# Casts of operands moved behind copies out of PSUM, and one set of block sums moved by one output block

## The chip, the cores and the metric

The kernel runs on one core of one Trainium2 chip. The metric is the device time of one execution in microseconds, as a median of several runs. One execution is also taken with the hardware profiler, and its trace gives the views that are quoted here.

## The reference, cut to what matters

Two layers over a stream `x` of 1024 tokens by 1024 channels. In layer 0 the output of two mixer branches goes through an output projection, is scaled by a gate and added to `x`. Layer 1 is the pooling mixer; in it stands most of what the change touches:

```python
def odd_mixer(h, p, on_grid):
    z = h @ p["w_in"]
    u, g = jnp.split(z, [W_POOL], axis=-1)          # 2048 columns each
    d = multiscale_pool(u ...)                      # windows of 2, 4, 8, 16 along a row of 64
    y = jnp.einsum("bngi,gij->bngj", d, p["w_grp"]) * p["scale"]
    return (y * jax.nn.silu(g)) @ p["w_out"]        # 2048 -> 1024

x = x + gate[:, None] * out_x                       # per layer
return rmsnorm(x, final_g)
```

All is float32, to float32 accuracy.

## The kernel before

**Layout.** Channels lie on the 128 partitions and tokens on the free axis, so a tile of 128 channels is 128x1024, in two halves of 512 (`HALF`). 1024 channels are 8 tiles (`KT`), the 2048 of the pooling mixer 16 (`NK`).

**Three products for one.** A float32 operand is cut into a high part, which is a cast to the fast format `fp32r` on ScalarE, and a low part, which is the operand less the high part, on VectorE (`split`, L101 to L103). `prod` (L985) multiplies high by high, high by low and low by high: 4 k-tiles by 3, 12 matmuls of 128x512 for a product.

**Seven products for eight.** From the output projection of layer 0 on, a pair of output column tiles is one block, made by `quad` (L1000). It treats weights and operand as 2x2 matrices of blocks and makes seven products (a Strassen-Winograd scheme). The operand's seven sums are called `BOPS = ("b11", "t1", "t2", "b21", "t3", "b22", "t4")`. `quad` issues the products in the order b11, t1, t2, b21, t3, b22, t4 into three PSUM banks `a`, `c` and `b` (in the trace `qa_`, `qc_`, `qb_` with the block's name). After the first, ScalarE copies `a` into `b` (L1005), because the products of t2, t3 and t4 are added on top of it. Wherever a part of the block is complete, `put(i, h, x, part)` takes it out of PSUM. For the second row of the block (`i == 1`) `put(1, 1, ...)` has to copy `b` out on ScalarE (L1483 in the gate blocks, `copied`, L1538, in the output blocks) before the product of t4 may go on adding to `b`. `keep_part` (L1031) copies first halves of sums into SBUF (L1033).

**The stages that matter here, in the order of the trace.** `woa` is the half of layer 0's output projection that goes over branch A: 4 blocks from about 686 us on, with operands `ya`. Then, for each pair of the 16 column tiles of the pooling mixer, a value block `v` and a gate block `g` (until about 1125 us). Then the output projection of the mixer in two parts of 1024 rows: blocks `wo0_0`, `wo0_2`, `wo0_4`, `wo0_6` with the operands of part 0 (`yops[0]`), and `wo1_0` and on with those of part 1.

**Operands of the mixer's output.** `y`, the mixer's values times the gate, comes out one pair of column tiles at a time. `y_keep` (L1405) stores the pair's blocks b11, b21 and b22 to memory; `y_sums` (L1410) makes t1 to t4 with four VectorE instructions (`block_sums`, L912 to L916) and stores them; `y_operand` (L1415) loads an operand again and splits it. `y_sums` of a pair runs one pair later; that of the last pair (14 and 15) runs inside a `put` of `wo0_0`.

**What sets the order.** A planner orders the instructions of each engine by a simulated time line and by priorities: an instruction's number in the program, less `EVAC = 1000` inside `tc.high_priority`. So what stands in a `put` is moved ahead of nearly all else when its inputs are there. `tc.issue_after(x)` puts the instructions that are written inside it behind `x` in the order of `x`'s engine. Each engine then works through its list in order. So does SP, which issues nearly all transfers: one that waits for a free tile holds up those behind it.

**Tiles that are shared.** Tiles come from pools with a fixed number of slots. The `d` pool has 16 tiles of 128x1024 and holds, around the first output blocks, the operands b11, b21 and t4 of part 0 (four tiles each), the last two column tiles y14 and y15, and weights. The `v` pool has two tiles of 128x512: the residuals of the output blocks' second row (`xp`, loaded at L1549) and the third sum of `y_sums` (`yt3`) take turns in it. A pair of raw weight tiles (`wr`) is loaded at L955 and freed when its splits are done. The ring gives block `wo0_2` the tiles wh, wl, d, d, wh, wl, d for its seven weight sums.

Of the kernel before, what the change touches and what calls it, by code (L numbers as in the profile page):

```python
# [55 lines left out]
def body(ctx, tc, xT, ctxT, cc, ccol, modT, modW, win, gw, wout, wu, grp, wg, wo1, small, edge, ident, outT):  # L56
    nc = tc.nc
# [849 lines left out]
    def split_op(ops, name, i, src):  # L907
        hi, lo = ops[name]
        return split(src, hi[i], lo[i], nc.vector)
# [87 lines left out]

    def quad(w, name, ops, put, ahead=None):  # L1000
        p1, p2, p3, p4, p5, p6, p7 = w
        a, c, b = psum(f"qa_{name}"), psum(f"qc_{name}"), psum(f"qb_{name}")
        prod(a, p1, ops["b11"], True, False)
        with tc.high_priority(offset=EVAC):
            evac = nc.scalar.copy(b, a)  # L1005
        prod(c, p5, ops["t1"], True, False)
        with tc.high_priority(offset=EVAC):
            put(1, 1, c, 0)
        prod(b, p6, ops["t2"], False, False)
        with tc.high_priority(offset=EVAC):  # L1010
            put(0, 1, b, 0)
        prod(a, p2, ops["b21"], False, True)
        with tc.high_priority(offset=EVAC):
            put(0, 0, a, None)
        w = None
        if ahead is not None:
            with tc.issue_after(evac.ins):
                w = ahead()
        prod(b, p7, ops["t3"], False, False)
        with tc.high_priority(offset=EVAC):  # L1020
            put(1, 1, b, 1)
        prod(c, p3, ops["b22"], False, True)
        with tc.high_priority(offset=EVAC):
            put(0, 1, c, 1)
        prod(b, p4, ops["t4"], False, True)
        with tc.high_priority(offset=EVAC):
            put(1, 0, b, None)
        return w


    def keep_part(parts, name, i, x):  # L1031
        parts[i] = ttile(f"s{i}_{name}")
        nc.scalar.copy(parts[i], x)  # L1033

    def wr_tile(name):
        return wpool.tile([P, D], F32, tag="wr", name=name)
# [214 lines left out]
    w0 = w0()  # L1251
    for name in BOPS[4:]:
        operand(ya, name, dtile, "ya")
        for i in range(KH):
            split_op(ya, name, i, kept[name][i])

    x1 = [None] * KT
    nacc = [atile("n1acc0"), atile("n1acc1")]
# [9 lines left out]
    def woa(m, w, ahead):  # L1268
        for q in range(2):
            x1[m + q] = xtile(f"x1_{m + q}")  # L1270

        def put(i, h, x, part):
            v, dr = x1[m + i][:, HALF[h]], x1_part[m + i][:, HALF[h]]
            if part != 1:
                nc.sync.dma_start(v, dr)
            nc.vector.scalar_tensor_tensor(out=v, in0=x, scalar=m0[:, 0, 2 * KT + m + i : 2 * KT + m + i + 1],
                                           in1=v, op0=mult, op1=add)
            if part != 0:
                nc.sync.dma_start(dr, v)
                square_acc(nacc[h][:, :H], v, (m, i) == (0, h), f"n1q{m}_{i}_{h}")  # L1280
        return quad(w, f"woa{m}", ya, put, ahead)

    idD = cH[:, :P]
    nc.sync.dma_start(idD, ident)
# [127 lines left out]
        for name in ("t1", "t2", "t3", "t4"):  # L1412
            y_store(m, name, t[name])

    def y_operand(ops, part, name, raw_tile, alloc):  # L1415
        hi, lo = [], []
        for q in range(2):
            if raw_tile is not None:
# [4 lines left out]
            if raw_tile is None:  # L1423
                r = lo[q].bitcast(F32)
                nc.sync.dma_start(r, y_raw[part][name][:, q * S : (q + 1) * S])
            split(r, hi[q], lo[q], nc.vector)
        halves = lambda ts: [t[:, h] for t in ts for h in HALF]
        ops[name] = halves(hi), halves(lo)

    yops = [{}, {}]  # L1430

    def y_operands(part, raws, names=BOPS, alloc=None):
        for name in names:
            y_operand(yops[part], part, name, next(raws),
                      alloc or (dtile if name in ("b11", "b21", "t4") else d2tile))

    def wo_ring(tags):
        def ring(name):
# [10 lines left out]
                     part == 1 and m >= KT - 4)  # L1449

    wo1_ring = wo_ring(iter(["x", "x", "x", "wh", "wl", "wh", "wl"] + ["wh", "wl", "d", "d"] * 14))
    vps, silu = [], [None]
    for m in range(0, NK, 2):
        wv = wv0 if m == 0 else v_weights(m, ring_x)
        if m == 0:
# [20 lines left out]
        def to_gate(i, h, x, part):  # L1476
# [3 lines left out]
                return  # L1480
            if part == 1:
                if i == 1:
                    nc.scalar.copy(v, x)  # L1483
                    x = v
                nc.vector.tensor_tensor(out=v, in0=x, in1=parts[i], op=add)
                x = v
# [16 lines left out]
                nc.sync.dma_start(raw, modT[1, n + q])  # L1503
                mod_tile(m1, 1, n + q, raw, (cL2,), raw)
        if m == NK - 2:
            y_operands(0, iter([dtile] + [xtile] * (4 - 1)), BOPS[:4])
        for i in range(2):
            for h in range(2):
                pool(m + i, h, vps[2 * i + h])
        w = quad(wq, f"g{m}", bx, to_gate, (lambda: wo1_weights(0, 0)) if m == NK - 2 else None)  # L1510
        if m == NK - 2:
            with tc.issue_after(silu[0].ins):
                y_operands(0, iter([xtile] * 7), BOPS[4:])
# [21 lines left out]

    def copied(name, x):
        t = ttile(f"b_{name}")
        nc.scalar.copy(t, x)  # L1538
        return t

    for m in range(0, KT, 2):
        parts = {}

        def put(i, h, x, part):
# [11 lines left out]
                x = s  # L1556
            gated(m + i, t, x)
            nc.sync.dma_start(x1_part[m + i][:, HALF[h]], t)
            if (m, i, h) == (0, 0, 1):
                y_sums(NK - 2)  # L1560
        def nxt():
            if m < KT - 2:
                with tc.issue_after(stored[0].ins):
                    return wo1_weights(0, m + 2)
            w = wo1_weights(1, 0)
            y_operands(1, iter([xtile]), BOPS[3:4])
            return w

        if m == KT - 2:
            with tc.issue_after(loaded[0].ins):  # L1570
                y_operands(1, iter([xtile] * 2), BOPS[1:3])
        w = quad(w, f"wo0_{m}", yops[0], put, nxt)
        if m == 2:
            with tc.issue_after(loaded[0].ins):
                y_operands(1, iter([xtile]), BOPS[:1], lambda name, dt: xtile(name, dt))
    def x2_load(m):
        with tc.issue_after(loaded[0].ins):
# [299 lines left out]
```

## Time and profile before

| | |
|---|---|
| median of 3 runs | 1294.53 us (1294.15 to 1294.73) |
| the profiled execution | 1297.47 us |
| its span, first to last instruction | 1295.7 us |
| TensorE (PE) busy | 1274.6 us |
| VectorE (DVE) busy | 1143.5 us |
| ScalarE (ACT) busy | 637.3 us |
| GpSimd (POOL) busy | 354.7 us |
| granted TensorE clock, mean | 0.996 |

The span runs from the first to the last instruction; the time of an execution has a little more round it. Busy time is the time in which an engine had an instruction in work. In a list of instructions a row is: start in us, duration in us, engine, line, operation, names written and read, shapes, and in square brackets how long the engine had stood idle before it and what ended that.

### The profile page before, as it was taken

The page shows a single profiled execution, that of the slowest core. Times are in us where ns is not written, and L with a number is a line of the kernel's source. Part 1 is how long each engine was busy: PE and PEld are TensorE (multiplying, and loading weights), DVE is VectorE, ACT ScalarE, POOL GpSimd, SP SyncE. Part 2 cuts the span into 40 slices and gives each one's busy share as a digit, 9 for nine tenths or more (in the row PEclk, how much of TensorE's full clock was granted, in tenths as well). Part 3 has the DMA queues.
Part 4 walks back from the last instruction along what each step waited for, and adds up shares of the span by engine and source line. Part 5 has one row for each costly group of instructions (what it writes and reads, how often), then busy time and mean ns, then how long its engine had stood idle before and what let it go on. Part 6 is the DMA issues. An engine that isn't in the chain of part 4 may idle for free.

```text
span 1295.7 us, 15787 instructions
## 1 busy us (share of the span) xinstructions
PE 1274.6 (98%) x5630; PEld 1025.1 (79%) x5630; DVE 1143.5 (88%) x1758; ACT 637.3 (49%) x936; POOL 354.7 (27%) x180
## 2 busy tenths in 40 slices
PE   9999999999999999999999999999999999999997
PEld 4468888888888888888887887788888888778786
DVE  6979999999999989998789758998989987877876
ACT  4343666566657633237335346744334444644543
POOL 3063655575657613543210022000000000000002
PEclk9999999999999999999999999999999999999998
DMA  9934111121112133532555356244233324868723
GB/s 365 359 117 151 58 41 66 41 74 42 65 41 90 66 106 119 179 141 85 169 194 200 111 191 192 75 153 155 90 122 130 122 106 147 276 211 271 283 80 130
DMA packets 82899, 181.80 MB, mean 140 GB/s; under 512 B 7810, under 2 KB 27650, under 8 KB 82820
## 3 DMA queue, kind: packets, MB, share of 16 engines
q1 hardware_dynamic: 74372, 176.60, 39.4%
q10 hardware_dynamic: 8448, 4.20, 1.1%
q8 instruction: 44, 0.72, 0.2%
q14 instruction: 35, 0.29, 0.1%
HBM read 136.72 MB, written 44.04 MB: 140 GB/s over the span
## 4 chain that ended last, share of the span: by engine, by line
PE 76%; DMA 10%; DVE 8%; ACT 3%; issue 2%; POOL 1%; SPq 0%; POOLq 0%; DVEq 0%; ACTq 0%
PE vg L501 7%; PE wob L501 7%; PE va L501 7%; PE gb L501 7%; PE xb L501 6%; PE g L501 4%; PE fold L281 3%; PE ga L135 2%; PE ga L501 2%; PE ga L134 2%; PE ga L133 2%; PE xbc L501 2%; DMA x_part<-xp 1%; DMA wr_wo<-wo 1%; DMA mod<-modT 1%
## 5 line engine op out<-in xcount | busy, mean ns | idle before, releaser
L501 DVE SCALAR_TENSOR_TENSOR conv<-u,sm,conv 128x505 f32<-128x505 f32 (+6 forms) x224 | 153.7, 745 | 0.9
L1678 POOL TENSOR_TENSOR o<-x,rr 128x256 f32<-128x256 f32 (+1 forms) x10 | 9.6, 993 | 445.0 <-ACT rr L1614 445.0
L501 POOL TENSOR_TENSOR l<-l,l 128x1280 f32<-128x1280 f32 (+1 forms) x23 | 63.9, 2795 | 91.9 <-DVE l L501 76.8
L501 ACT ACTIVATE l<-g,sm 128x512 f32<-128x512 f32 (+1 forms) x96 | 58.5, 618 | 57.6 <-PE g L501 55.9
L281 PE MATMUL fold<-graw,wu 128*128 128x512 f32 x128 | 56.6, 603 | 0.0
L102 ACT CAST wq_g<-wr_g 128x512 fp32r<-128x512 f32 x48 | 28.2, 620 | 56.3 <-DVE wr_g L970 23.1
L501 PE MATMUL wob<-ybh,wh_wob 128*128 128x512 f32 x128 | 50.7, 396 | 0.0
L501 PE MATMUL gb<-h0h,wl_gb 128*128 128x512 f32 x128 | 49.9, 390 | 0.1
L501 PE MATMUL vg<-h0h,wl_vg 128*128 128x512 f32 x128 | 50.0, 391 | 0.0
L501 PE MATMUL gb<-h0h,wh_gb 128*128 128x512 f32 x128 | 49.9, 390 | 0.0
L501 PE MATMUL gb<-h0l,wh_gb 128*128 128x512 f32 x128 | 49.9, 390 | 0.0
L501 PE MATMUL wob<-ybh,wl_wob 128*128 128x512 f32 x128 | 49.9, 390 | 0.0
L501 PE MATMUL vg<-h0h,wh_vg 128*128 128x512 f32 x128 | 49.9, 390 | 0.0
L501 PE MATMUL vg<-h0l,wh_vg 128*128 128x512 f32 x128 | 49.8, 389 | 0.0
L501 PE MATMUL va<-h0h,wl_va 128*128 128x512 f32 x128 | 49.8, 389 | 0.0
L501 PE MATMUL va<-h0l,wh_va 128*128 128x512 f32 x128 | 49.8, 389 | 0.0
L501 PE MATMUL va<-h0h,wh_va 128*128 128x512 f32 x128 | 49.8, 389 | 0.0
L501 PE MATMUL wob<-ybl,wh_wob 128*128 128x512 f32 x128 | 49.8, 389 | 0.0
L501 DVE TENSOR_TENSOR_SCAN l<-l,l 128x256 f32<-128x256 f32 (+1 forms) x32 | 48.7, 1521 | 1.1
L103 POOL TENSOR_TENSOR wl_wu<-wr_wu,wh_wu 128x1024 fp32r<-128x1024 f32 x8 | 19.2, 2395 | 108.7 <-ACT wh_wu L102 108.1
L102 ACT CAST wq_v<-wr_v 128x512 fp32r<-128x512 f32 x48 | 28.2, 619 | 41.9 <-DMA wr_v<-wfold 16.5
L281 PEld LDWEIGHTS fold<-graw,wu 128*128 128x128 f32 x128 | 24.7, 195 | 29.9 <-issue 28.9
(611 smaller groups left out, 4361.0 us busy)
## 6 DMA issues: line engine op xcount, KB each, us to landing
mod<-modT SPq DMA_DIRECT2D x20, 512.0 KB, 5.8
x_part<-xp SPq DMA_DIRECT2D x32, 256.0 KB, 3.0
mod<-modT SPq DMA_DIRECT2D x32, 256.0 KB, 3.1
wr_v<-wfold SPq DMA_DIRECT2D x16, 512.0 KB, 3.6
wr_g<-wg SPq DMA_DIRECT2D x16, 512.0 KB, 4.3
wr_wo<-wo SPq DMA_DIRECT2D x16, 512.0 KB, 5.3
y_b<-y SPq DMA_DIRECT2D x24, 256.0 KB, 4.0
y_t<-y SPq DMA_DIRECT2D x24, 256.0 KB, 3.2
```

Source lines behind the costliest of these rows:

```text
L102: return (nc.scalar.copy(hi, src), eng.tensor_tensor(out=lo, in0=src, in1=hi.bitcast(F32), op=sub))
L103: eng.tensor_tensor(out=lo, in0=src, in1=hi.bitcast(F32), op=sub))
L133: nc.tensor.matmul(ps, hi[:, kc], xh[k][:, cols], start=(k == 0), stop=False)
L134: nc.tensor.matmul(ps, hi[:, kc], xl[k][:, cols], start=False, stop=False)
L135: nc.tensor.matmul(ps, lo[:, kc], xh[k][:, cols], start=False, stop=(k == ks - 1))
L281: nc.tensor.matmul(ps, w[:, kc], gs[i], start=(i == 0), stop=(i == 3))
L501: last[eng] = f(*args, **kw)
L1678: nc.gpsimd.tensor_tensor(out=outs[k // per][:, k % per], in0=x1[k][:, cols], in1=rr, op=mult)
```

## The change

`held_back(steps)` is new. It runs the given steps behind the ScalarE instruction that `left[0]` holds, and `left[0]` is now set at each copy out of PSUM by `quad`, `keep_part`, L1483 and `copied`. `quad` calls it at two places: for `first` behind the copy of `a` into `b`, and for `last` behind `put(1, 1, b, 1)`. Only the splits are held back so; the loads stay where they were. Four operands go this way:

- t4 of `ya`, as `first` of block `woa0`;
- b21 of part 0, as `last` of the last gate block `g14`;
- b21 of part 1, as `last` of `wo0_6` (its list `last_op` is filled by `nxt` within the block);
- b11 of part 1, whose splits now also stand behind the last such copy of `wo0_2`;

(the first three through `held_back`, the fourth through `issue_after`; b21 of part 0 and of part 1 have two wide casts each, b11 of part 1 two, t4 of `ya` four of half the width). Besides, `y_sums(NK - 2)` moves from the `put` of block `wo0_0` to the same `put` of block `wo0_2`.

```diff
--- before.py
+++ after.py
@@ -997,12 +997,13 @@
 
 
 
-    def quad(w, name, ops, put, ahead=None):
+    def quad(w, name, ops, put, ahead=None, first=(), last=()):
         p1, p2, p3, p4, p5, p6, p7 = w
         a, c, b = psum(f"qa_{name}"), psum(f"qc_{name}"), psum(f"qb_{name}")
         prod(a, p1, ops["b11"], True, False)
         with tc.high_priority(offset=EVAC):
-            evac = nc.scalar.copy(b, a)
+            left[0] = evac = nc.scalar.copy(b, a)
+        held_back(first)
         prod(c, p5, ops["t1"], True, False)
         with tc.high_priority(offset=EVAC):
             put(1, 1, c, 0)
@@ -1019,6 +1020,7 @@
         prod(b, p7, ops["t3"], False, False)
         with tc.high_priority(offset=EVAC):
             put(1, 1, b, 1)
+        held_back(last)
         prod(c, p3, ops["b22"], False, True)
         with tc.high_priority(offset=EVAC):
             put(0, 1, c, 1)
@@ -1028,9 +1030,16 @@
         return w
 
 
+    left = [None]
+
+    def held_back(steps):
+        with tc.issue_after(left[0].ins):
+            for step in steps:
+                step()
+
     def keep_part(parts, name, i, x):
         parts[i] = ttile(f"s{i}_{name}")
-        nc.scalar.copy(parts[i], x)
+        left[0] = nc.scalar.copy(parts[i], x)
 
     def wr_tile(name):
         return wpool.tile([P, D], F32, tag="wr", name=name)
@@ -1251,8 +1260,10 @@
     w0 = w0()
     for name in BOPS[4:]:
         operand(ya, name, dtile, "ya")
-        for i in range(KH):
-            split_op(ya, name, i, kept[name][i])
+        splits = [lambda i=i, name=name: split_op(ya, name, i, kept[name][i]) for i in range(KH)]
+        if name != "t4":
+            for s in splits:
+                s()
 
     x1 = [None] * KT
     nacc = [atile("n1acc0"), atile("n1acc1")]
@@ -1278,7 +1289,7 @@
             if part != 0:
                 nc.sync.dma_start(dr, v)
                 square_acc(nacc[h][:, :H], v, (m, i) == (0, h), f"n1q{m}_{i}_{h}")
-        return quad(w, f"woa{m}", ya, put, ahead)
+        return quad(w, f"woa{m}", ya, put, ahead, splits if m == 0 else ())
 
     idD = cH[:, :P]
     nc.sync.dma_start(idD, ident)
@@ -1412,7 +1423,7 @@
         for name in ("t1", "t2", "t3", "t4"):
             y_store(m, name, t[name])
 
-    def y_operand(ops, part, name, raw_tile, alloc):
+    def y_operand(ops, part, name, raw_tile, alloc, later=None):
         hi, lo = [], []
         for q in range(2):
             if raw_tile is not None:
@@ -1423,16 +1434,20 @@
             if raw_tile is None:
                 r = lo[q].bitcast(F32)
                 nc.sync.dma_start(r, y_raw[part][name][:, q * S : (q + 1) * S])
-            split(r, hi[q], lo[q], nc.vector)
+            step = lambda r=r, q=q: split(r, hi[q], lo[q], nc.vector)
+            if later is None:
+                step()
+            else:
+                later.append(step)
         halves = lambda ts: [t[:, h] for t in ts for h in HALF]
         ops[name] = halves(hi), halves(lo)
 
     yops = [{}, {}]
 
-    def y_operands(part, raws, names=BOPS, alloc=None):
+    def y_operands(part, raws, names=BOPS, alloc=None, later=None):
         for name in names:
             y_operand(yops[part], part, name, next(raws),
-                      alloc or (dtile if name in ("b11", "b21", "t4") else d2tile))
+                      alloc or (dtile if name in ("b11", "b21", "t4") else d2tile), later)
 
     def wo_ring(tags):
         def ring(name):
@@ -1449,7 +1464,7 @@
                      part == 1 and m >= KT - 4)
 
     wo1_ring = wo_ring(iter(["x", "x", "x", "wh", "wl", "wh", "wl"] + ["wh", "wl", "d", "d"] * 14))
-    vps, silu = [], [None]
+    vps, silu, last_op = [], [None], []
     for m in range(0, NK, 2):
         wv = wv0 if m == 0 else v_weights(m, ring_x)
         if m == 0:
@@ -1480,7 +1495,7 @@
                 return
             if part == 1:
                 if i == 1:
-                    nc.scalar.copy(v, x)
+                    left[0] = nc.scalar.copy(v, x)
                     x = v
                 nc.vector.tensor_tensor(out=v, in0=x, in1=parts[i], op=add)
                 x = v
@@ -1503,11 +1518,12 @@
                 nc.sync.dma_start(raw, modT[1, n + q])
                 mod_tile(m1, 1, n + q, raw, (cL2,), raw)
         if m == NK - 2:
-            y_operands(0, iter([dtile] + [xtile] * (4 - 1)), BOPS[:4])
+            y_operands(0, iter([dtile] + [xtile] * 2), BOPS[:3])
+            y_operands(0, iter([xtile]), BOPS[3:4], later=last_op)
         for i in range(2):
             for h in range(2):
                 pool(m + i, h, vps[2 * i + h])
-        w = quad(wq, f"g{m}", bx, to_gate, (lambda: wo1_weights(0, 0)) if m == NK - 2 else None)
+        w = quad(wq, f"g{m}", bx, to_gate, (lambda: wo1_weights(0, 0)) if m == NK - 2 else None, last=last_op)
         if m == NK - 2:
             with tc.issue_after(silu[0].ins):
                 y_operands(0, iter([xtile] * 7), BOPS[4:])
@@ -1535,9 +1551,10 @@
 
     def copied(name, x):
         t = ttile(f"b_{name}")
-        nc.scalar.copy(t, x)
+        left[0] = nc.scalar.copy(t, x)
         return t
 
+    last_op = []
     for m in range(0, KT, 2):
         parts = {}
 
@@ -1556,22 +1573,22 @@
                 x = s
             gated(m + i, t, x)
             nc.sync.dma_start(x1_part[m + i][:, HALF[h]], t)
-            if (m, i, h) == (0, 0, 1):
+            if (m, i, h) == (2, 0, 1):
                 y_sums(NK - 2)
         def nxt():
             if m < KT - 2:
                 with tc.issue_after(stored[0].ins):
                     return wo1_weights(0, m + 2)
             w = wo1_weights(1, 0)
-            y_operands(1, iter([xtile]), BOPS[3:4])
+            y_operands(1, iter([xtile]), BOPS[3:4], later=last_op)
             return w
 
         if m == KT - 2:
             with tc.issue_after(loaded[0].ins):
                 y_operands(1, iter([xtile] * 2), BOPS[1:3])
-        w = quad(w, f"wo0_{m}", yops[0], put, nxt)
+        w = quad(w, f"wo0_{m}", yops[0], put, nxt, last=last_op)
         if m == 2:
-            with tc.issue_after(loaded[0].ins):
+            with tc.issue_after(loaded[0].ins), tc.issue_after(left[0].ins):
                 y_operands(1, iter([xtile]), BOPS[:1], lambda name, dt: xtile(name, dt))
     def x2_load(m):
         with tc.issue_after(loaded[0].ins):
```

## The prediction

> **What bounds the kernel now.** I read the page first, then the list of TensorE's waits, then short windows round those waits, then ScalarE's, VectorE's and SP's instructions in order of time.
>
> ```profile
> PE 1274.6 (98%) x5630; PEld 1025.1 (79%) x5630; DVE 1143.5 (88%) x1758; ACT 637.3 (49%) x936; POOL 354.7 (27%) x180
> ```
>
> TensorE is busy for 1274.6 of 1295.7 us. Its instructions are the same before and after, so a reordering can win only what TensorE now spends waiting, and the waits can be listed. This is the list of its waits over the whole span (total, times, longest), in part:
>
> ```profile
> PE ms_n L207 <- DVE dg_n L204: 2.3, 1, 2.3
> PE qb_wo L989 <- ACT b_wo L1538: 1.5, 2, 1.1
> ...
> PE qc_wo L992 <- DVE wq_wo L103: 1.0, 1, 1.0
> ...
> PE qb_g L989 <- ACT y L1483: 0.9, 1, 0.9
> ...
> PE qb_woa L989 <- ACT qb_woa L1005: 0.4, 1, 0.4
> PE qc_wo L989 <- DVE xp L1532: 0.3, 1, 0.3
> ```
>
> The last five rows lie in five windows of 4 us, which hold 4.16 us of idle TensorE together (columns: length, then busy time of PE, PEld, DVE, ACT, POOL, the granted clock, DMA share, GB/s); the sixth row is what follows them, and the seventh the window of the 2.3 us wait:
>
> ```profile
> 690.00:694.00 4.00, 3.59 (x16) 2.67 (x15) 4.00 (x8) 3.83 (x8) 0.00 (x0) 1.00 0.83 273
> 1121.00:1125.00 4.00, 3.11 (x14) 2.23 (x14) 4.00 (x6) 2.74 (x6) 0.00 (x0) 1.00 0.63 188
> 1145.00:1149.00 4.00, 2.67 (x11) 1.58 (x10) 4.00 (x7) 2.59 (x5) 0.00 (x0) 1.00 0.55 204
> 1162.00:1166.00 4.00, 3.60 (x17) 2.64 (x16) 4.00 (x7) 3.93 (x7) 0.00 (x0) 1.00 0.19 67
> 1201.00:1205.00 4.00, 2.86 (x13) 2.06 (x12) 4.00 (x6) 3.95 (x6) 0.00 (x0) 1.00 1.01 387
> ```
>
> ```profile
> 1220.00:1260.00 40.00, 40.00 (x178) 33.15 (x177) 32.49 (x50) 22.27 (x38) 0.00 (x0) 1.00 0.29 106
> ```
>
> ```profile
> 750.00:800.00 50.00, 47.60 (x213) 38.35 (x212) 30.68 (x39) 24.76 (x34) 19.16 (x8) 1.00 0.60 198
> ```
>
> From 1220 to 1260 TensorE does not stop, so time won ahead of it should reach the end whole. A stop costs more than the wait that is named:
>
> ```profile
> 1121.73 0.39 PE L992 MATMUL qa_wo<-y_b11h,wq_wo 128*128 128x512 f32 x1
> 1123.01 0.50 PE L989 MATMUL qb_g<-x_t4h,wq_g 128*128 128x512 f32 x1 [0.89 <-ACT y L1483]
> 1123.35 0.40 PE L991 MATMUL qb_g<-x_t4l,wq_g 128*128 128x512 f32 x1
> ```
>
> Matmuls in a stream start 0.23 us apart. Here 1.28 us pass, 1.05 over the pace, and the next start comes 0.34 later, 0.11 over it: 1.16 us for a wait of 0.89, so 0.27 beyond each wait. The stops are therefore A at 692: 0.4 + 0.27 = 0.68; B at 1122: 1.16; C at 1145: two waits, 0.33 + 1.00 + 0.54 = 1.87; D at 1163: 0.40 + 0.27 = 0.67; E at 1202: 1.14 + 0.27 = 1.41. All five together are 5.8 us. That is the ceiling of the change, 0.45% of the run.
>
> **The change part by part.** It adds and removes no instruction and no byte; every price is one of place. The four held-back groups come first.
>
> Stop A. TensorE waits for the copy of the first product into the second accumulator (L1005), which stands behind two casts of t4:
>
> ```profile
> 690.40 0.61 ACT L102 CAST wq_woa<-wr_woa 128x512 fp32r<-128x512 f32 x1
> 690.92 1.14 ACT L102 CAST ya_t4h<-u 128x512 fp32r<-128x512 f32 x2
> 691.97 0.57 ACT L1005 COPY qb_woa<-qa_woa 128x512 f32<-128x512 f32 x1
> ```
>
> Without them the copy starts at 690.92, 1.05 us sooner, against 0.58 that TensorE is short. Gain 0.68. The casts' cover: t4 is the last of the seven products, each 12 matmuls or 2.7 us, so they have over 10 us.
>
> Stop B. The copy at L1483 stands behind both wide casts of part 0's b21:
>
> ```profile
> 1119.16 1.05 ACT L102 CAST y_b21h<-yr_b 128x1024 fp32r<-128x1024 f32 x1 [0.48 <-DMA yr_b<-y_b]
> 1120.42 1.05 ACT L102 CAST y_b21h<-yr_b 128x1024 fp32r<-128x1024 f32 x1 [0.20 <-DMA yr_b<-y_b]
> ...
> 1121.90 0.59 ACT L1487 ACTIVATE y<-qa_g 128x512 f32<-128x512 f32 x1
> 1122.38 0.57 ACT L1483 COPY y<-qb_g 128x512 f32<-128x512 f32 x1
> ```
>
> With 2.1 us of casts gone from ahead of it, the copy is in time for the 1.05 us over the pace. Gain 1.16. What is late next are the b21 casts themselves: three products (8.2 us) lie between the copy and their first use, and the casts and their subtractions on VectorE need 2.1 + 1.2 of it. If that cover went, the fourth product of the block would wait.
>
> [...]
>
> Stop D. The copy at L1538 stands behind one cast of part 1's b11 and four casts of weights:
>
> ```profile
> 1160.37 1.05 ACT L102 CAST y_b11h<-yr_b 128x1024 fp32r<-128x1024 f32 x1 [4.12 <-DMA yr_b<-y_b]
> 1161.32 0.62 ACT L102 CAST wq_wo<-ws_wo 128x512 fp32r<-128x512 f32 x1
> 1161.84 1.66 ACT L102 CAST wq_wo<-wr_wo 128x512 fp32r<-128x512 f32 x3
> 1163.40 0.57 ACT L1538 COPY b_wo<-qb_wo 128x512 f32<-128x512 f32 x1
> ```
>
> The change takes only the first away. The weight casts wait for a load, whose arrival releases VectorE at 1159.09 (row below). B and C put TensorE here about 3 us sooner, and the load does not come 3 us sooner. Bounds: 0.67 won, or nothing. I take nothing.
>
> Stop E. The same copy, behind one cast of part 1's b21:
>
> ```profile
> 1200.94 1.15 ACT L102 CAST wq_wo<-wr_wo 128x512 fp32r<-128x512 f32 x2 [1.18 <-DVE wr_wo L977]
> 1201.99 1.04 ACT L102 CAST y_b21h<-yr_b 128x1024 fp32r<-128x1024 f32 x1
> 1202.93 0.57 ACT L1538 COPY b_wo<-qb_wo 128x512 f32<-128x512 f32 x1
> ```
>
> The copy moves up to 1201.99, by 0.94. I take 0.94 of the 1.41; the rest belongs to the two weight casts. The held casts have two products, over 5 us, before the block that follows reaches its b21.
>
> Stop C and the sums. The last column tiles' sums (four VectorE instructions and four stores) now carry block 0's place. They are pulled forward as soon as their tile can be had:
>
> ```profile
> 1128.50 0.68 DVE L913 TENSOR_TENSOR yt<-y,y 128x512 f32<-128x512 f32 x1
> ...
> 1142.38 0.69 DVE L969 TENSOR_TENSOR ws_wo<-wr_wo,wr_wo 128x512 f32<-128x512 f32 x1 [1.45 <-DMA wr_wo<-wo]
> ```
>
> ```profile
> 1159.09 0.69 DVE L969 TENSOR_TENSOR ws_wo<-wr_wo,wr_wo 128x512 f32<-128x512 f32 x1 [1.38 <-DMA wr_wo<-wo]
> ```
>
> They cost two things. Four times 0.68 = 2.7 us lie among the subtractions that free the weights' raw buffers, on a VectorE that does not pause. And SP stands in line (its waits between 1120 and 1165, then its issues):
>
> ```profile
> SPq L1549 <- DMA y_t<-yt: 2.7, 1, 2.7
> ```
>
> ```profile
> 1129.20 0.32 SPq L1400 DMA_DIRECT2D y_t<-yt  x1
> ...
> 1135.27 0.32 SPq L1549 DMA_DIRECT2D xp<-x_part  x1
> 1135.68 0.38 SPq L955 DMA_DIRECT2D wr_wo<-wo  x1
> ```
>
> The sums hold one of the two `v` tiles, a residual load (L1549) waits 2.7 us for the store of that tile, and the second weight load for block 2 is queued behind it. It lands just ahead of 1142.38, and C's wait of 1.00 us is for these weights. With the sums a block later, the residual takes the `v` tile at once, SP does not wait there, and the raw buffer is free up to 2.7 us sooner. C's 1.27 (1.00 + 0.27) then goes, and of the other 0.60, a drain by VectorE, about half: 1.5 us.
>
> What the move adds. The sums ask for a `v` tile in turn behind block 0's residuals, so I expect them near 1150, and their 2.7 us of VectorE and four issues of 0.32 us on SP stand in front of block 4's weights. SP's wait of 2.7 us goes with them. The tiles of y14 and y15 stay in the pool of 16 `d` tiles: 12 hold part 0's operands, 2 hold y14 and y15, 2 are left for three weight tiles of block 2, so the third waits until the first one's product is done and keeps a raw buffer longer. No row shows this. Bounds: nothing, as that product is over some 10 us before the third tile is used, or the 2.7 us wait shifted whole to block 4. The nearest row is the 1.38 us that VectorE already waits for block 4's load at 1159.09, so I take something below it, 0.8.
>
> The sum: 0.68 + 1.16 + 1.5 + 0 + 0.94 − 0.8 = 3.5 us. The profiled execution took 1297.47 us round its span of 1295.7; it becomes 1294.0. It lies 2.94 above the median of the runs, 1294.53, so the median becomes 1291.0. A change of 0.2%, 2.6 us, is about what a measurement of this kernel tells from none.
>
> **Rivals.** *Half of it stays.* A and B have their copies freed of all that they need; C, D and E share their delay with loads. If block 4's late weights take back what C gives, and the planner puts other ready casts ahead of E's copy, A + B = 1.8 us are left: 1292.7, inside 0.2%. For it speaks that all four windows from 1121 show VectorE full (4.00), so work taken away from one place is work added to the next; against it, that each freed copy had the cast directly ahead of it or within two instructions. The case in which a re-planned order opens as much elsewhere as it closes, so that nothing is seen (1294.5), belongs here.
>
> *Held tiles stop TensorE.* This one ends slower. If the sums run only where they now stand in the code, behind the sixth product of block 2 (VectorE near 1161.2), they end at 1163.9, and the tile for the seventh product's weights comes free when a store has landed:
>
> ```profile
> y_t<-y SPq DMA_DIRECT2D x24, 256.0 KB, 3.2
> ```
>
> ```profile
> DMA to landing us min/median/max: 2.6/4.9/8.9
> ```
>
> (the second row is for the residuals' transfers). With 3.2 to 8.9 us of landing, 0.62 for a cast and 0.68 for its subtraction, TensorE goes on at 1168.4 to 1174.1 and not at 1163.6: 4.8 to 10.5 us. Less A, B, C and E (4.3) that is +0.5 to +6.2, about 1297.9 in the middle. It decides from a stop of 7 us on. Against it: the first weight tile's slot is free by then.
>
> In this rival alone the clock could count. A wait of 2.3 us left it at 1.00 in the window from 750. [...]
>
> **How the numbers follow.** Forecast (2.6 to 5.8 us won): 0.60, its own range 1288.7 to 1291.9. Half or nothing: 0.31. Held tiles: 0.09. So faster 0.60, same 0.31, slower 0.09. The range runs from the ceiling (1288.7) to 1295.6, which takes in the second case up to a loss of 1 us.
>
> **What would show it.** Right: the four waits on L1005, L1483 and twice L1538 gone or under 0.3 us; the sums on VectorE after 1145; no wait of L1549 for the sums' store in block 0; the second weight load of block 2 issued by 1134. Wrong: a new wait of the products in block 2 or 4 on weights (L103), a wait of SP on L1549 for the sums' store in block 2, or D's stop grown; or the order from 700 to 1100 changed, with waits that are not in the list above.

## The result, and the profile after

| kernel | median, us (range, runs) | ratio to before, 95% interval |
|---|---|---|
| before, with the result | 1294.15 (1291.34 to 1297.33, 7) | |
| changed, with the result | 1302.27 (1298.22 to 1418.11, 7) | 1.0063 [1.0045, 1.0081] |
| changed, second time | 1296.95 (1295.30 to 1303.22, 12) | 1.0021 [1.0007, 1.0036] |
| changed, third time | 1297.81 (1295.27 to 1303.54, 12) | 1.0032 [1.0014, 1.0051] |

The change makes the kernel slower, by 0.2 to 0.6%; the forecast was 1291.0, 0.3% faster. The profiled one of the seven ran at a granted clock of 0.85 (1418.11 us) and counts in no ratio, so the profile after is that of the changed kernel's second set (1298.65 us, span 1296.9). The other six of the seven have a mean of 1301.8, against 1298.1 in the two later sets; none of the six was profiled, so what they lost more stays open.

```profile
PE 1277.1 (98%) x5630; PEld 1026.0 (79%) x5630; DVE 1141.1 (88%) x1758; ACT 637.8 (49%) x936; POOL 354.4 (27%) x180
```

The same five windows as in the prediction, then two more (length, busy time of PE, PEld, DVE, ACT, POOL, granted clock, DMA share, GB/s):

```profile
690.00:694.00 4.00, 3.92 (x18) 2.93 (x17) 4.00 (x8) 3.82 (x8) 0.00 (x0) 1.00 0.85 285
1121.00:1125.00 4.00, 4.00 (x19) 3.31 (x18) 4.00 (x6) 4.00 (x7) 0.00 (x0) 1.00 0.74 293
1145.00:1149.00 4.00, 4.00 (x19) 3.34 (x18) 3.62 (x7) 1.11 (x2) 0.00 (x0) 1.00 0.57 198
1162.00:1166.00 4.00, 3.98 (x18) 2.92 (x17) 4.00 (x6) 3.53 (x6) 0.00 (x0) 1.00 0.60 203
1201.00:1205.00 4.00, 4.00 (x20) 3.30 (x19) 0.43 (x1) 0.00 (x0) 0.00 (x0) 1.00 1.00 299
1130.00:1134.00 4.00, 2.14 (x9) 1.35 (x8) 2.16 (x3) 2.38 (x4) 0.00 (x0) 0.97 1.00 386
1206.00:1210.00 4.00, 2.30 (x11) 1.56 (x10) 2.33 (x3) 3.40 (x5) 0.00 (x0) 1.00 1.04 420
```

The five windows held 4.17 us of idle TensorE before, by their rows, and hold 0.10 now: in this execution all five listed stops are gone. The last two windows show where TensorE stops instead. Its instructions there, and ScalarE's (start, length, engine, line, operation; in brackets the idle time before it and what ended it):

```profile
1133.67 0.71 PE L989 MATMUL qc_wo<-y_b22h,wq_wo 128*128 128x512 f32 x1 [1.86 <-ACT y_b22h L102]
...
1208.18 0.50 PE L989 MATMUL qb_wo<-y_t4h,wq_wo 128*128 128x512 f32 x1 [1.70 <-ACT b_wo L1554]
```

```profile
1131.62 1.04 ACT L102 CAST y_t4h<-yr_t 128x1024 fp32r<-128x1024 f32 x1 [2.75 <-DMA yr_t<-y_t]
1132.57 1.04 ACT L102 CAST y_b22h<-yr_b 128x1024 fp32r<-128x1024 f32 x1
...
1206.60 1.04 ACT L102 CAST y_t3h<-y_t3l 128x1024 fp32r<-128x1024 f32 x1 [7.06 <-DMA y_t3l<-y_t]
1207.55 0.58 ACT L1554 COPY b_wo<-qb_wo 128x512 f32<-128x512 f32 x1
```

At 1133 TensorE waits for b22's cast, which stands behind a cast of t4 that waits 2.75 us for its load. At 1208 it waits for the copy of block 6 (L1554, L1538 of before), which stands behind the first cast of part 1's t3; ScalarE sat idle for 7.06 us in that cast's wait.

The sums did move, and SP's wait for their store in block 0 went (VectorE, then SP):

```profile
1147.33 0.69 DVE L913 TENSOR_TENSOR yt<-y,y 128x512 f32<-128x512 f32 x1 [0.38 <-DMA x_part<-xp]
```

```profile
1129.15 0.94 SPq L955 DMA_DIRECT2D wr_wo<-wo  x2
```

Both weight loads of block 2 are issued by 1130.1, where the second stood at 1135.68.

**A measure for what follows.** *Lost time* of a profile is the sum, over TensorE's instructions that start between 1110 and 1262 us, of what the time from the start of the one before exceeds 0.23 us by (excesses over 0.1 us; waits, restarts and half clock together). One execution's profile gives one number:

| order of the work from 1110 on | lost, us, one for each profile |
|---|---|
| before | 5.3, 4.5, 1.8, 3.2 |
| changed | 7.4, 7.4, 7.6, 7.7 |
| four holds, sums as before | 3.4, 2.6 |
| three holds (without part 0's b21), sums as before | 1.3, 2.7 |
| sums moved, no hold | 5.5, 4.9 |
| sums moved, part 1's t3, b22, t4 held | 5.0 |
| changed, part 1's t3, b22, t4 held too | 5.3 |
| the same, part 0's b21 not held | 4.4, 2.4 |

Changed minus before is 7.5 − 3.7 = 3.8 us, close to the 3.4 between the means of the runs (24 of changed in its later two sets, 1298.1; 150 of before beside the experiments, 1294.7). In the rows with two or four profiles the last is of a kernel that has one more edit far ahead, at 770 to 815 us ("roots first", below).

### The profile page after: what moved, and what is told of

It is laid out like the page before. It is cut to its first block, busy times and chain, and to the rows that moved or that the text cites. A ratio compares the mean times of both kernels' runs of the same rounds, so it can differ in the third digit from the quotient of the medians.

```text
span 1416.3 us, 15794 instructions
## 1 busy us (share of the span) xinstructions
PE 1403.5 (99%) x5630; PEld 1052.5 (74%) x5630; DVE 1140.5 (81%) x1758; ACT 637.5 (45%) x936; POOL 349.2 (25%) x180
## 4 chain that ended last, share of the span: by engine, by line
PE 98%; ACT 1%; POOL 0%; DVE 0%; issue 0%; POOLq 0%; ACTq 0%
PE wob L501 7%; PE va L501 7%; PE vg L501 7%; PE gb L501 7%; PE xb L501 6%; PE fold L281 5%; PE g L501 4%; PE qb_v L989 2%; PE ga L133 2%; PE qb_g L992 2%; PE qb_v L992 2%; PE ga L135 2%; PE ga L501 2%; PE qb_g L989 2%; PE qb_v L991 2%; PE qb_g L991 2%
## 5 line engine op out<-in xcount | busy, mean ns | idle before, releaser
L281 PE MATMUL fold<-graw,wu 128*128 128x512 f32 x128 | 65.5, 679 | 0.0
L501 PE MATMUL wob<-ybh,wh_wob 128*128 128x512 f32 x128 | 54.3, 424 | 0.0
L501 PE MATMUL vg<-h0l,wh_vg 128*128 128x512 f32 x128 | 53.7, 419 | 0.0
L501 PE MATMUL va<-h0l,wh_va 128*128 128x512 f32 x128 | 53.7, 419 | 0.0
L501 PE MATMUL wob<-ybl,wh_wob 128*128 128x512 f32 x128 | 53.6, 419 | 0.0
L501 PE MATMUL gb<-h0l,wh_gb 128*128 128x512 f32 x128 | 53.6, 419 | 0.0
L501 PE MATMUL va<-h0h,wh_va 128*128 128x512 f32 x128 | 53.4, 417 | 0.0
L501 PE MATMUL gb<-h0h,wh_gb 128*128 128x512 f32 x128 | 53.4, 417 | 0.0
L501 DVE SCALAR_TENSOR_TENSOR conv<-cL,wsum,conv 128x506 f32<-128x506 f32 (+3 forms) x70 | 47.5, 745 | 0.2
L103 POOL TENSOR_TENSOR wl_wu<-wr_wu,wh_wu 128x1024 fp32r<-128x1024 f32 x8 | 19.1, 2392 | 115.5 <-ACT wh_wu L102 113.6
L501 POOL TENSOR_TENSOR l<-l,uc 128x1280 f32<-128x1280 f32 x16 | 47.1, 2966 | 0.0
```

Of the source, the lines that this page charges most:

```text
L103: eng.tensor_tensor(out=lo, in0=src, in1=hi.bitcast(F32), op=sub))
L281: nc.tensor.matmul(ps, w[:, kc], gs[i], start=(i == 0), stop=(i == 3))
L501: last[eng] = f(*args, **kw)
```

## The experiments

**The parts alone.** First the changed kernel again.

> The changed kernel once more, for a profile in which TensorE's clock is granted in full (the profile shown with the result was granted 0.85). Theory 'sums': the re-planned blocks wo0_2 to wo0_6 stop TensorE for 10 to 13 us at full clock, since the four copies win about 3 and the time is 8 longer; these waits stand between 1125 and 1210 us, on weights (L103) or on held tiles. Theory 'clock': there are fewer waits than before, under 3 us between 690 and 1210, but the granted clock is lower somewhere (mean 0.990 to 0.994 against 0.996), which accounts for the time. Time by both: 1300 to 1304.

Measured: 1296.95, in the table above. Then the holds alone, the sums in their old place:

```
-            if (m, i, h) == (2, 0, 1):
+            if (m, i, h) == (0, 0, 1):
                 y_sums(NK - 2)
```

> Only the casts are held behind the copies; the sums of the last column tiles stay in block wo0_0. Theory 'sums': the copies' gain alone, 2 to 3.5 us faster than before (1291 to 1292.5). Theory 'clock': the fewer stops, the lower the clock, so slower than before by some 3 to 8 us (1297 to 1302).

1294.27, ratio 1.000 [0.9986, 1.0014]: no difference, to within 1.8 us either way. The opposite edit in the kernel before, the sums alone:

> Only the sums of the last column tiles move from block wo0_0 to wo0_2; no cast is held back. Theory 'sums': all of the loss and more, 8 to 12 us slower than before (1302 to 1306), with new waits of TensorE from 1125 to 1210. Theory 'clock': about as before or slower by up to 4 us (1294 to 1298), as only stop C goes.

1298.89, ratio 1.0030 [1.0016, 1.0045]. The kernel before against itself:

> The kernel before, sent as a kernel of its own, to see how far the same program differs from itself and what clock it is granted from run to run. Theory 'sums': 1294 within 1 us, clock 0.996. Theory 'clock': 1294 as well, but with runs whose clock differs by 0.002 or more and whose time follows the clock.

1294.45, ratio 1.0002 [0.9987, 1.0017]. The theory that fewer stops lower the granted clock fell: it was 0.994 to 0.997 in all four. The profile of the last showed something else, in its list of waits:

```profile
PE qb_wo L989 <- ACT s_wo L1033: 1.9, 1, 1.9
PE qb_woa L989 <- ACT qb_woa L1005: 1.9, 1, 1.9
```

Of the five stops of the prediction A is in it, nearly five times as long (1.9 us against 0.4); B, C and D are not, E is too short for the list, and a stop at L1033 is there that the first profile of before did not have. The order of the instructions is the same in both. ScalarE ahead of that copy, in the first profile and in this one:

```profile
1130.81 1.06 ACT L102 CAST y_t4h<-yr_t 128x1024 fp32r<-128x1024 f32 x1
...
1133.67 0.57 ACT L1033 COPY s_wo<-qb_wo 128x512 f32<-128x512 f32 x1
```

```profile
1128.25 1.05 ACT L102 CAST y_t4h<-yr_t 128x1024 fp32r<-128x1024 f32 x1 [0.98 <-DMA yr_t<-y_t]
...
1131.23 1.04 ACT L102 CAST y_t4h<-yr_t 128x1024 fp32r<-128x1024 f32 x1 [0.98 <-DMA yr_t<-y_t]
1132.18 0.58 ACT L1033 COPY s_wo<-qb_wo 128x512 f32<-128x512 f32 x1
```

Here both casts of t4 wait 0.98 us for their loads, and the copy stands behind them; in the first profile they did not wait. A third profile of before has a stop at L1033 too (below). With one order of instructions the stops differ, here by two loads that the casts wait for, 0.98 us each.

**The t3 cast.** New theory ("queue"): the loss is the t3 cast ahead of the copy of block 6. In the changed order the first product of the second half stands ahead of that copy, so its copy (L1005) releases t3's casts early, and E's place ahead of L1554, from which b21 was moved, goes to a cast whose load is still under way. The edit puts t3's, b22's and t4's casts behind the copy; `hold` is the copy of block 6:

```
             if m == 0:
-                y_operands(1, iter([None] * 3), BOPS[4:])
+                steps = []
+                y_operands(1, iter([None] * 3), BOPS[4:], later=steps)
+                with tc.issue_after(hold.ins):
+                    for step in steps:
+                        step()
```

> The changed kernel once more, on the chip on which the next two are compared with it. Both theories: slower than before by 0.2 to 0.6%, 1297 to 1302 us where before takes 1294.5. Theory 'queue': TensorE stops near 1208 us for the copy of block 6 of the first half (L1554), and ScalarE stands idle just ahead of it in a cast of part 1's t3 that waits for its load; that stop is 1.5 to 4 us long. Theory 'weights': the largest stop after 1100 us stands between 1130 and 1170, at weights or operands, and the one near 1208 is under 1 us.

> The changed kernel with one edit more: the casts of part 1's t3, b22 and t4 are put behind the copy of block 6 (L1554) in ScalarE's order; their loads stay where they are, and the sums stay a block later. Theory 'queue' (the loss is the t3 cast that waits for its load ahead of this copy): no stop at the copy near 1208, and the time falls by 1.5 to 4 us against the changed kernel, to within 1.3 us of before (1293.2 to 1295.8 where before takes 1294.5). Theory 'weights' (the loss is the new order of loads and products in blocks 2 and 4): the time stays within 0.7 us of the changed kernel.

> The kernel before with the sums one block later, no cast group held back but part 1's t3, b22 and t4, which stand behind the copy of block 6. With the sums alone the kernel was slower by 0.30%. Theory 'queue': within 0.1% of before. Theory 'weights': 0.2 to 0.4% slower still, with stops between 1130 and 1170 us.

Changed: 1297.81 (1.0032, above). With the edit 1296.44, ratio 1.0016 [0.9997, 1.0035]; sums alone with the edit 1295.29, 1.0012 [0.9992, 1.0033]. The changed kernel stopped 2.7 us at L1554 again; with the edit the longest wait there or at its like is 0.5:

```profile
PE qc_wo L989 <- ACT y_b22h L102: 1.3, 1, 1.3
PE qa_wo L992 <- DVE wq_wo L103: 0.9, 1, 0.9
PE qb_wo L989 <- ACT b_wo L1554: 0.7, 2, 0.5
```

The stop goes, and the median falls by 1.4 us, which the overlapping intervals do not tell from nothing; a wait for weights (L103) is new. "Queue" is half of the story at most. In the same set, the sums in their old place in the code but with a tile of their own, which was to test step C:

```
-        t = block_sums(*y_blocks(m), vtile(f"yt3_{m}"), nc.vector)
+        own = ttile(f"yt3_{m}") if m == NK - 2 else vtile(f"yt3_{m}")
+        t = block_sums(*y_blocks(m), own, nc.vector)
```

> The kernel before with the sums in their old place, but their first result in a tile of the pool that holds ScalarE's copies and not in one of the two tiles that the residuals also use. This takes away SP's wait for the sums' store alone. By step C of the prediction: SP's wait at L1549 of 2.7 us goes, the second weight load of block 2 is issued by 1134 us and the time falls by about 1 us. By theory 'weights': no gain, since what the weights win at block 2 they lose at block 4. If stops come and go with the arrival of transfers, no difference that can be measured (within 0.1%).

1296.93, ratio 1.0024 [1.0004, 1.0045]: no gain, a small loss. SP's wait for the sums' store is not among its waits any more, and block 2's two weight loads are issued together at 1126.77, yet the time does not fall. Its one profile is of the shortest of its runs (1292.53, lost 3.8), so it can't show the loss. It does show that the edit did more than it was meant to: the planner put the sums 8 us later (1136.7, before 1128.5), and TensorE's own order is another. Counted place by place over the 5630 matmuls, 372 of them have other tiles than in before. So it is with every kernel whose sums moved (358 in the changed kernel, up to 380 in others), and not with the holds (17 with four, 10 with three). In the new order of this kernel and of the sums alone, t1's product of block 4 comes behind t2's and no longer covers the copy of `a` into `b` that t2 waits for:

```profile
PE qb_wo L989 <- ACT qb_wo L1005: 1.4, 1, 1.4
```

In before no such stop is listed. The own-tile kernel is therefore no clean test of step C.

**The other new stop.** Part 0's b21 is put back ahead of the copy at L1483, once with the three other holds alone, once in the changed kernel with t3 held:

```
-            y_operands(0, iter([dtile] + [xtile] * 2), BOPS[:3])
-            y_operands(0, iter([xtile]), BOPS[3:4], later=last_op)
+            y_operands(0, iter([dtile] + [xtile] * 3), BOPS[:4])
```

> Three of the four cast groups held back (t4 in the out projection of the first half, part 1's b11, part 1's b21); part 0's b21 casts keep their old place ahead of the copy at L1483, and the sums keep their old place too. With all four groups the time was that of before (1294.27), and TensorE stopped near 1135 to 1140 for b22's casts, which stand behind b21's. Theory 'it changes sides': the b21 casts, once held back, only make b22's late; without that hold the stops for b22 near 1133 to 1140 (1.0 to 2.6 us) go, the stop at 1122 for the copy (1.2 us) comes back, and the time is 0.5 to 1.5 us below before, 1293.0 to 1294.0. Rival: the holds are worth nothing in any place, because the stops follow the arrival of transfers: 1294.0 to 1295.2, no difference from before.

> The changed kernel with part 1's t3, b22 and t4 behind the copy of block 6, and with part 0's b21 casts back in their old place ahead of the copy at L1483. With the first edit alone the time was 1296.44, and TensorE stopped 1.5 us near 1140 for b22's cast. Theory 'it changes sides': this stop goes, one of about 1.2 us at 1122 comes back, and the time falls by 0.3 to 1.5 us, to 1295.0 to 1296.2. Rival 'nothing in any place': 1296.0 to 1297.0. If it is at or below before (1294.5 or less), both moves of the sums' place and the holds are free, and the whole loss of the change was the two casts.

> One more profile of the kernel before, to see which of its stops are there each time. Theory 'stops belong to the order of the instructions': the copy at L1005 near 692, the one at L1483 near 1122 and the copies at L1538 each show over 0.3 us. Theory 'stops follow the arrival of transfers': at least two of the five listed in the prediction are missing, as in the second profile, and the fold's stop near 786 (ms_n) has another length than 2.3 us; a stop of over 2.5 us there is followed by about 3.4 us or more of half clock, one under 1.6 us by none.

> A third profile of the changed kernel. Theory 'queue': the stop at the copy of block 6 (L1554) near 1208, behind the cast of part 1's t3 that waits for its load, is there again with 1.5 to 4 us, and the one for b22's cast near 1135 with 1.3 to 2 us. Rival: one of the two is missing or under 0.5 us, and then they are scatter and not the change's.

Three holds: 1294.50, ratio 1.0007 [0.9985, 1.0028]. Changed, both mended: 1295.12, ratio 1.0004 [0.9982, 1.0025]. A further profile of the changed kernel (1298.08) has both stops again, a further one of before (1295.29) only A and E of the five, waits of 0.36 and 0.12, and again the one at L1033. Changed, then before:

```profile
PE qc_wo L989 <- ACT y_b22h L102: 1.8, 1, 1.8
PE qb_wo L989 <- ACT b_wo L1554: 1.8, 2, 1.1
...
PE ms_n L207 <- DVE dg_n L204: 3.1, 1, 3.1
...
PE qb_wo L989 <- ACT s_wo L1033: 1.0, 1, 1.0
```

So the two new stops belong to the change: all its profiles have both, and TensorE stops in none of before's for b22 or for that copy behind t3. But before's own runs spread over 10 us, and an edit worth 1 us could not be told.

**Where the spread comes from.** The stage with the largest difference between profiles, 41.9 to 48.8 us, is the fold ahead of layer 1 (770 to 815). ScalarE in the longest one (changed, t3 held), then TensorE's wait and the windows behind it:

```profile
784.60 0.59 ACT L261 COPY fo<-fold 128x512 f32<-128x512 f32 x1 [5.01 <-DMA wfold<-fo]
...
787.44 0.26 ACT L201 ACTIVATE rc_n<-ms_n,eps_r 128x4 f32<-128x4 f32 x1
```

```profile
PE ms_n L207 <- DVE dg_n L204: 4.1, 1, 4.1
```

```profile
788.00:790.00 2.00, 0.86 (x1) 0.50 (x2) 1.64 (x3) 0.88 (x2) 0.54 (x1) 0.50 0.18 53
790.00:792.00 2.00, 2.00 (x5) 1.13 (x4) 1.07 (x3) 1.39 (x3) 1.60 (x1) 0.50 0.69 242
792.00:794.00 2.00, 2.00 (x6) 1.20 (x4) 2.00 (x5) 1.05 (x1) 1.53 (x2) 0.50 0.86 233
```

A copy waits 5.01 us for a store to land; the norm's square root stands behind it; VectorE's `dg` and TensorE wait for the root; then TensorE runs at half clock (0.50 from 788 to 794). It is the same kind of order as at the casts, in another place. One edit puts the roots ahead of that copy and of one cast of weights (`root_op` is the activation of L201). TensorE's order stays the same to the last instruction:

```
+                if (g, kp, s) == (2, 1, 1):
+                    with tc.issue_after(root_op[0].ins):
+                        nc.scalar.copy(o, ps)
...
+                    if (g, kp) == (3, 0):
+                        wctx.enter_context(tc.issue_after(root_op[0].ins))
```

> The kernel before with one other edit: in the fold's stage the square roots (L201) stand ahead of the copy of the fold's fourth result, which waits for a store, and ahead of the cast of the next weights, in ScalarE's order; the sums and the five operands stay in their old places. Three profiles of before show at ms_n near 786 a wait of 2.3, under 0.2 and 3.1 us, and the stage from the norm's sums to the first product of v takes 44.6, 41.9 and 46.8 us. Theory 'most of what one execution differs from another by, and the half clock that follows, comes from this wait on a store': the wait at ms_n is under 0.5 us, the stage takes 41.5 to 43 us with no half clock in it, the time falls by 1 to 3 us and its scatter (2.2 to 3.5 us) narrows. Rival 'the stage is held by its transfers in any order': another instruction of TensorE waits in its place, the stage still takes 42 to 49 us, and the time stays within 0.1%.

> The same edit in the kernel with three of the four cast groups held back and the sums in their old place (1294.50 without it, same as before). If the scatter of the fold's stage is taken away, what the three holds bring can be seen: theory 'the holds free their copies of what they need': 1 to 2 us below the kernel before with the roots first. Theory 'the stops follow the arrival of transfers': within 0.7 us of it.

Roots first: 1293.96 (1292.12 to 1295.95), ratio 0.9989 [0.9970, 1.0007]; the wait at `ms_n` is gone, the stage takes 42.1 us, and the standard deviation of 12 runs is 1.2 us where before has 3.6 in the same set. ScalarE there:

```profile
778.16 0.26 ACT L203 ACTIVATE rc_n<-ms_n,eps_r 128x4 f32<-128x4 f32 x1 [0.42 <-PE ms_n L202]
...
780.49 0.59 ACT L270 COPY fo<-fold 128x512 f32<-128x512 f32 x1
```

With the three holds as well 1292.90 (1291.39 to 1294.49), deviation 0.9. On this quiet kernel the rest could be told apart:

> The whole change (four holds, sums one block later) on the kernel with the roots first, which takes 1293.96 us with a scatter of 1.2. Theory 'two casts' (the change loses at part 1's t3 cast ahead of the copy of block 6 and at b22's casts behind b21's, some 1.2 to 2.9 and 1.3 to 2 us a time, more with half clock): 2 to 4 us slower than the roots first alone, 1296 to 1298. Rival 'the change is neutral and what was seen is scatter of the fold's stage': within 0.7 us, 1293.3 to 1294.7.

> The four holds alone, sums in their old place, roots first. With three of the holds it took 1292.90. Theory 'b21's hold changes sides' (the copy at L1483 comes in time and b22's casts come late): 0.3 to 1.7 us above three holds, 1293.2 to 1294.6. By step B of the prediction the hold wins 1.2 us: 1291.7.

> The sums one block later alone, no hold, roots first. Theory 'two casts' with step D grown (part 1's b11 cast and block 4's weights ahead of the copy in block 2, 2 us in both profiles of such kernels; part 1's t3 cast ahead of the copy of block 6): 2 to 4 us above the roots first alone, 1296 to 1298. By step C of the prediction, 0.7 us below it: 1293.3.

> The change with its two new stops mended (part 1's t3, b22 and t4 behind the copy of block 6; part 0's b21 back in its old place), roots first. Theory 'two casts': what the change lost is back, 1293 to 1294.5, 2 to 4 us below the whole change with the roots first. If the sums' new place also brings what step C said, it lies 0.7 us below three holds, at 1292.2. Rival 'the later weights of block 4 and of the second half cost as much': 1295 or more.

| with the roots first | median, us (12 runs) | means: against roots first alone, 95% |
|---|---|---|
| alone | 1293.96 | |
| three holds | 1292.90 | −1.0 ± 0.9 |
| four holds | 1293.77 | +0.3 ± 1.0 |
| sums moved | 1295.97 | +1.9 ± 1.1 |
| the whole change | 1297.28 | +3.3 ± 1.1 |
| the change, two stops mended | 1295.10 | +1.4 ± 1.1 |

(The first two sets ran on another chip than the other four; before was at 1294.87 and 1294.18 on them. What the chips differ by, 0.5 ± 1.7 by the means of before, is in none of the intervals that compare across them.) The change costs 3.3 us with the fold's scatter out of the way. Part 0's b21 hold costs 1.3 ± 0.9 (four against three holds). Mending the two stops brings 2.0 ± 1.2, on one chip. What the sums' move costs beyond them, 2.4 ± 1.0 against three holds, no profile pins down: three profiles of the changed kernel with t3 held behind the copy show D's stop (0.7, 0.8, 0.7 lost) and, two of them, 1.1 and 1.2 us for weights of the second half (L103) that come late. It stays open. Three holds with the roots first is the best kernel here: below the changed kernel on every run, and 1.9 ± 0.7 us below the mean of all 150 runs of before, on several chips; against the 22 runs beside it the ratio is 0.9989 [0.9972, 1.0005], so that it beats before is likely and not settled.

## Why the prediction was wrong

**Its ceiling.** The step "the stops are therefore A ... E" took the waits of one execution for a property of the order. In three more profiles of this order (one with the roots first) B, C and D are missing, and E is 0.2, 0.3 and 0.4. The 5.8 us were there in one execution: 5.1 of them lie behind 1110 us, where before loses 5.3, 4.5, 1.8 and 3.2 us, most of the last three at the copy of L1033 or in the half clock behind it (in the second a stop of 1.9 us and 1.7 us of clock, in the third a stop of 1.0).

**A (0.68).** The casts of t4 went from ahead of the copy, and the stop moved: with the hold, profiles show 0.3 to 0.7 us at 697 to 699 for ya_t2h's cast and 0.4 behind it, which those without the hold do not. In one profile with the hold (four holds, roots first) the copy itself still comes 1.07 us late, behind a cast of b22 and one of weights. It wins nothing that can be seen.

**B (1.16).** Here "what is late next are the b21 casts themselves" failed; it looked at TensorE's order only. A held cast also holds its raw buffer, for which t4's load waits. Four holds (SP's wait and load; ScalarE: the copy of L1483 under its line there, then the casts), and then three holds, without part 0's b21:

```profile
SPq L1442 <- DVE y_b21l L103: 2.7, 2, 2.0
```

```profile
1125.22 0.80 SPq L1442 DMA_DIRECT2D yr_t<-y_t  x2
```

```profile
1120.40 0.58 ACT L1509 COPY y<-qb_g 128x512 f32<-128x512 f32 x1
...
1132.00 1.05 ACT L102 CAST y_t4h<-yr_t 128x1024 fp32r<-128x1024 f32 x1 [2.73 <-DMA yr_t<-y_t]
1132.96 1.04 ACT L102 CAST y_b22h<-yr_b 128x1024 fp32r<-128x1024 f32 x1
```

```profile
1120.47 0.38 SPq L1442 DMA_DIRECT2D yr_t<-y_t  x1
```

```profile
1119.45 0.58 ACT L1509 COPY y<-qb_g 128x512 f32<-128x512 f32 x1
...
1127.78 1.06 ACT L102 CAST y_t4h<-yr_t 128x1024 fp32r<-128x1024 f32 x1
1128.73 1.04 ACT L102 CAST y_b22h<-yr_b 128x1024 fp32r<-128x1024 f32 x1
```

SP waits for b21's subtraction in both (with three holds 2.5 us in all), but there it is an earlier load that waits, here t4's first. Counted from the copy, t4's first load goes out at 4.8 us instead of 1.0, its cast waits 2.73 us, and b22's cast behind it starts at 12.6 instead of 9.3: the copy has two casts' length (2.1) less ahead of it, and b22 comes 3.3 later. TensorE's stop for b22 is in every profile with this hold and in none without it. So the 2.1 us of casts changed sides, and the price was higher there: four holds against three cost 1.3 ± 0.9 us.

**C (1.5).** The mechanism was right (sums at 1147, no wait of SP, weights sooner), the price was not: in the three other profiles of before's order TensorE does not stop near 1145, so there is nothing to win there. The own-tile kernel had the larger part of the step (no wait of SP, weights sooner) without a gain, but TensorE's order is another in it.

**D (0).** Right for the changed kernel (nothing, 0.8, 0.9, nothing). Without the hold of part 1's b11 the moved sums made it 2.1, 2.0 and 1.1.

**E (0.94).** The copy's place was freed; the step that failed is that nothing else would take it. In the changed kernel the planner puts t3's cast there (1.7, 2.7, 1.1 and 1.2 us of wait in the four profiles). It does so with the sums alone too, but there TensorE, in yet another order, does not stop for that copy. With the sums in place E is won: none of the four profiles with part 1's b21 held and the sums in place stops there.

**What the move adds (0.8, up to 2.7).** Mis-sized and in the wrong place: 1.9 ± 1.1 alone, 3.0 ± 1.1 on top of the four holds. The prediction priced weights and tiles; it did not ask what the re-planned order would put ahead of the copies, and that TensorE's own order of products would be re-planned with it. Its "half of it stays" rival named the first ("the planner puts other ready casts ahead of E's copy"); the cast was not ready. How much of the loss is due to TensorE's new order no run separates.

**The clock.** "In this rival alone the clock could count" failed: the price of 0.27 beyond a wait leaves out the half clock that follows some of them: in the changed kernel's second set 3.40 us of it behind the wait of 1.86 at 1133, and none behind that of 1.70 at 1208.

## What to carry to other kernels

Before the stops of a profile are added up, look at a second profile of the same kernel: only the ones in every profile belong to the order (here B, C and D were in one of four). Holding an instruction back also holds its input buffer and every later load for that buffer (here t4's first load went out 4.8 us after the copy and not 1.0), and the freed place goes to the next instruction that the planner has, which may be one that waits (here t3's cast, with ScalarE idle for 7.06 us). Moving one group of instructions can re-plan the order of engines that it does not run on (here 358 of TensorE's 5630 matmuls), so compare the orders of all engines before a single wait is priced. Where executions scatter by more than the effect, find the stage that scatters and quiet it first; here that cost one edit, and 12 runs then told 1 us.

## What was not expected of the hardware

Some short stops were followed by a stretch of half clock. Two like stops at 1134, in the changed kernel with the roots first and in that without:

```profile
1132.00:1134.00 2.00, 0.74 (x2) 0.55 (x3) 1.71 (x2) 2.00 (x4) 0.00 (x0) 0.77 1.00 406
1134.00:1136.00 2.00, 2.00 (x6) 1.56 (x6) 2.00 (x3) 2.00 (x3) 0.00 (x0) 0.50 0.32 131
...
1132.00:1134.00 2.00, 0.16 (x2) 0.07 (x1) 1.04 (x1) 2.00 (x3) 0.00 (x0) 1.00 0.98 359
1134.00:1136.00 2.00, 2.00 (x8) 1.44 (x9) 2.00 (x4) 2.00 (x3) 0.00 (x0) 1.00 0.69 273
```

The wait of 2.39 us halved the clock, that of 1.84 did not. Over all profiles, ahead of the last stage: no wait of up to 1.70 us did (eight of 1.3 or more); of nine between 1.82 and 2.30, five did and four did not (1.84, 1.93, 2.01 and 2.30); all six from 2.39 up did. In each case with half clock, windows of 1 us add up to 3.40 to 3.42 us of it, 1.7 us of clock lost, or, after the two longest waits (3.27 and 4.12), to 6.84 us, a loss of 3.4. So stops from 1.8 us on had to be counted here. What decides between like stops no run shows.
